# Gated differential attention on one core: two elementwise steps moved from VectorE to GpSimd

## The chip, the cores and the metric

The program runs on one core of a Trainium2 chip. A core has five engines that work side by side and wait for each other through semaphores: TensorE (PE, matmul; PEld is its weight load), VectorE (DVE), ScalarE (ACT), GpSimd (POOL) and SyncE (SP, which here only issues DMAs). Each engine works through its own instructions in one fixed order. The metric is device time in microseconds for one execution. Before the change it is 1170.07 us, the median of 3 runs (1167.32 to 1170.65).

## The reference

The layer is one pre-norm residual block over x (1024 tokens, width 1024). With 16 heads, each of two 64-wide query and key halves and 128-wide values:

```python
h = rms_norm(x, norm_g)
q, k, v, z = jnp.split(h @ w_in, 4, axis=-1)          # each 2048 wide
q = rms_norm(q.reshape(b, s, 16, 2, 64), q_norm_g) * 64 ** -0.5
k = rms_norm(k.reshape(b, s, 16, 2, 64), k_norm_g)
probs = softmax(q k^T - slope * distance, causal)      # two maps per head
o = (probs[:, :, 0] - lam * probs[:, :, 1]) @ v        # 128 wide per head
o = rms_norm(o, head_norm_g) * (1.0 - lam_0)
o = o.reshape(b, s, 2048) * jax.nn.silu(z)
return x + o @ w_out
```

The change touches two places: how w_in is prepared for TensorE, and the last product of a head, rms_norm(o, head_norm_g) * (1 - lam_0) * silu(z).

## The kernel before

**Numbers in two parts.** TensorE is fed 16-bit operands. Each fp32 matrix is split in a high part (the rounded value) and a low part (what the rounding left), and a product is three matmuls: high by high, high by low, low by high. So w_in has to be scaled and split before a head can be projected.

**Stages.** A prologue loads x, norms and transposes it, and prepares the first head's weights. Then the program goes through 16 heads (odd ones first). While head i is projected (`project`), head i-1 is attended (`attend`); `merge` interleaves the two generators by planned times, and a scheduler then orders each engine's instructions. At the end come the last gates and the output projection.

**`project`.** For each of 8 token blocks, 24 matmuls of 384 columns into `pg` (q, k and v together; lines 365 to 367). ACT copies `pg` to `rw` and `vh`, DVE makes `vl` (line 419). For each half of the tokens `norm` works on q and k: GpSimd multiplies q by a gain (line 380), DVE sums squares (L378), adds an eps (L95), scales (L383) and makes the low part (L387), and DMA transposes to `qk`. Then for each half of the tokens `gate` runs 24 matmuls of 512 columns into `pz` (lines 442 to 444), and a chain of ACT and DVE makes silu(z) in the tile `sz`: Exp L447, min L448, Ln L449, L450, Exp L451, and L452, which multiplies by `inv`, the factor that undoes the weights' scaling. `pg` and `pz` share three PSUM banks, so a new `pg` may have to wait until L452 has read an old `pz`.

**`split_w`.** The next head's w_in comes as `raww` (128 partitions, 8 pieces of the contraction, 4 blocks q, k, v, z of 128 columns). There is one buffer of it. ACT squares the blocks for their scale (L159), the scale is worked out in small steps, ACT writes the high parts (L197, one per block), and the low parts follow: for the blocks in `LO_POOL` (v and z) on GpSimd as a scaling in place (L200) and a subtraction (L201); for the others (q and k) on DVE in one instruction (L203). The next head's `raww` DMAs (L135, on SP's queue) can be issued when the last of these has read the buffer.

**`attend`.** 8 steps, one for each block of 128 queries. A step's scores go into `pss`, which has four PSUM banks: two maps, each in pieces of up to 512 keys (L564). DVE evacuates each piece with the bias added (L553), ACT takes Exp (L570), DVE combines the two maps (L576), ACT and DVE split the result (L66, L580), a DMA transposes it into `wt` (L582). After step 5 the first four blocks are multiplied by the values, the second four in the next head's stretch (L594 to L596). Each gives a tile of 512 tokens: `os`, its squares `sq`, and a split `sqh`, `sql` (GpSimd, L607) that TensorE sums over the partitions with two matmuls into `pmn` (L613, L614). ACT turns the sum into 1/rms (L616, L617), DVE multiplies `os` by the gain `gh` and by it (L624), and `finalize` multiplies by `sz` on GpSimd (L532) and stores to `g_dram`. Heads 10, 12 and 14 (`LATE`) get their gates at the very end; 10 and 12 use line 622 for their norm, and 14, the last, does its products on DVE.

Of the kernel before, what the change touches and what calls it, by code (L numbers as in the profile page):

```python
# [9 lines left out]
F32 = mybir.dt.float32  # L10
# [4 lines left out]
ALU = mybir.AluOpType  # L15
# [17 lines left out]
NORM_AT = 6  # L33
TAIL = (0, 1, 1, 0, 0, 0, 0, 0)
PSS, PSG = 4, 3
LO_POOL = (2, 3)


@with_exitstack
def diff_attention_kernel(  # L40
# [67 lines left out]
    with ExitStack() as main:  # L108
# [31 lines left out]
        def split_w(raw, blocks, wt, hd, first=False, pin=lambda ins: ins):  # L140


            if "both" not in wt:
                wt["both"] = wp.tile([P, 2, KT, 4, P], F16, name="wsp", tag="wsp")
                wt["hi"], wt["lo"] = wt["both"][:, 0], wt["both"][:, 1]
                wt["inv"] = wsm.tile([P, 2, 4], F32, name="inv", tag="inv", bufs=3)
            hi, lo, inv = wt["hi"], wt["lo"], wt["inv"]
            n, bs = len(blocks), slice(blocks[0], blocks[-1] + 1)
            bd = wsm.tile([P, 4], F32, name="bd", tag="bd")
            if first:  # L150
                b8 = wsm.tile([P, 3, KT], F32, name="b8", tag="b8", bufs=1)
                for k in range(KT):
                    pin(V.tensor_reduce(out=b8[:, :, k], in_=raw[:, k, bs], axis=AX.X, op=ALU.max,
                                        apply_absolute_value=True))
                    yield
                pin(V.tensor_reduce(out=bd[:, :n], in_=b8, axis=AX.X, op=ALU.max))
            else:
                for j, s_ in enumerate(blocks):
                    A.activation(hi[:, :, s_], raw[:, :, s_], AF.Square, accum_out=bd[:, j:j + 1])  # L159
                    yield  # L160
            br = wsm.tile([P, 4], F32R, name="br", tag="br")
            if n % 2:
                G.memset(br.bitcast(F32), 0.0)
            pin(V.tensor_scalar(br[:, :n], bd[:, :n], 1.0, None, ALU.mult))
            while wt["pb"] is None:
                yield
            pb = wt["pb"]()
            T.matmul(pb[:, :n + n % 2], ones, br[:, :n + n % 2], start=True, stop=True)
            top = wsm.tile([P, 4], F32, name="topw", tag="topw")
            top = top[:, :n]  # L170
            pin(V.tensor_scalar(top, pb[:, :n], float(P), 2.0 ** (-20 if first else -40), ALU.mult, ALU.max))
            if not first:
                A.activation(top, top, AF.Ln)
                A.activation(top, top, AF.Exp, scale=0.5)
            pin(V.tensor_scalar(top.bitcast(I32), top.bitcast(I32), 0x7F800000, None, ALU.bitwise_and))
            sc = wsm.tile([P, 4], F32, name="scw", tag="scw")
            sc = sc[:, :n]
            pin(V.reciprocal(sc, top))
            pin(V.tensor_scalar(sc, sc, 2.0 ** 14, None, ALU.mult))

            def rest():

                V.tensor_scalar(inv[:, 0, bs], top, sg[1], 2.0 ** -14, ALU.mult, ALU.mult)
                V.tensor_scalar(inv[:, 1, bs], inv[:, 0, bs], -1.0, None, ALU.mult)
                if blocks[0] == 0 and not isinstance(hd, slice):
                    ep = wsm.tile([P, 2], F32, name="ep", tag="ep")
                    V.tensor_tensor(ep, sc[:, :2], sc[:, :2], ALU.mult)
                    V.tensor_scalar(ep, ep, sg[2], unit_of(hd) ** 2, ALU.mult, ALU.mult)
                    wt["ep"] = ep

            if not first:
                rest()
            yield
            for ks in (slice(0, 4), slice(4, 8)) if first else (slice(0, 8),):
                for j, s_ in enumerate(blocks):
                    src, h_, l_, c_ = raw[:, ks, s_], hi[:, ks, s_], lo[:, ks, s_], sc[:, j:j + 1]
                    pin(A.activation(h_, src, AF.Copy, scale=c_))  # L197
                    yield
                    if s_ in LO_POOL:
                        pin(G.tensor_scalar(src, src, c_, 1.0, ALU.mult, ALU.mult))  # L200
                        pin(G.tensor_tensor(l_, src, h_, ALU.subtract))  # L201
                    else:
                        pin(V.scalar_tensor_tensor(out=l_, in0=src, scalar=c_, in1=h_,  # L203
                                                   op0=ALU.mult, op1=ALU.subtract))
                    yield
            if first:
                rest()

        def unit_of(hd):
            return 2.0 ** ((8 - (hd + 2) // 2) // 2 - 11)  # L210
# [3 lines left out]
        with ExitStack() as pro:  # L214
# [52 lines left out]
            for t in range(NB):  # L267
# [18 lines left out]
                if t == 4:  # L286
# [12 lines left out]
                    gh = cp.tile([P, 1], F32, name="gh")  # L299
                    Q.dma_start(gh, head_norm_g[:, None])  # L300
                    V.tensor_scalar(gh, gh, 1.0 - LAM0, None, ALU.mult)

                    V.tensor_tensor(gk, gain[:, 0], gk, ALU.mult)
                    ga = x1.tile([P, 64], F32, name="ga")
# [133 lines left out]
        def gate(st, wt, n, c):  # L438

            pz = ps_g.tile([P, 512], F32, name="pz", tag="pg")  # L440
            for k in range(KT):
                T.matmul(pz, wt["hi"][:, k, n], hh[c][:, k], start=k == 0, stop=False)  # L442
                T.matmul(pz, wt["hi"][:, k, n], hl[c][:, k], start=False, stop=False)  # L443
                T.matmul(pz, wt["lo"][:, k, n], hh[c][:, k], start=False, stop=k == KT - 1)  # L444
                yield k
            e = vp.tile([P, 512], F32, name="sz", tag="sz", bufs=3)
            A.activation(e, pz, AF.Exp, scale=wt["inv"][:, 1, n:n + 1])  # L447
            V.tensor_scalar(e, e, 1e18, None, ALU.min)  # L448
            A.activation(e, e, AF.Ln, bias=1.0)  # L449
            V.scalar_tensor_tensor(out=e, in0=pz, scalar=wt["inv"][:, 1, n:n + 1], in1=e, op0=ALU.mult, op1=ALU.max)  # L450
            A.activation(e, e, AF.Exp, scale=-1.0)  # L451
            V.scalar_tensor_tensor(out=e, in0=pz, scalar=wt["inv"][:, 0, n:n + 1], in1=e,  # L452
                                   op0=ALU.mult, op1=ALU.mult)
            st["z"].append(e)

# [79 lines left out]
        def attend(hd, st):  # L535
# [48 lines left out]
            def values(c, t):  # L584
# [20 lines left out]
                A.activation(sqh, os, AF.Square)  # L605
                sql = tmp.tile([P, 512], F32R, name="sql", tag="sql")
                e.tensor_tensor(sql, sq, sqh.bitcast(F32), ALU.subtract)  # L607
                pos["n"] = (os, sq, sqh, sql)

            def head_norm(c):  # L610
# [7 lines left out]
                if hd in LATE[:-1]:  # L618
                    nm = ("whz", "wlz")[c]
                    t1 = wzp.tile([P, 512], F32, name="t1", tag=nm)  # L620
                    st["t"].append(t1)
                    V.scalar_tensor_tensor(out=t1, in0=os, scalar=gh, in1=sq, op0=ALU.mult, op1=ALU.mult)
                else:
                    V.scalar_tensor_tensor(out=sq, in0=os, scalar=gh, in1=sq, op0=ALU.mult, op1=ALU.mult)  # L624
                    finalize(hd, c, sq, st["z"][c])

            ts = []
# [119 lines left out]
```

## Time and profile before

| | us |
|---|---|
| median of 3 runs | 1170.07 |
| the profiled execution's own time | 1169.15 |
| its span in the trace | 1167.4 |
| PE busy | 1109.9 (95%) |
| DVE busy | 906.5 (78%) |
| ACT busy | 751.7 (64%) |
| POOL busy | 269.7 (23%) |

The prediction is made against the profiled execution's own time, 1169.15 us. A matmul counts as busy until its last result is out, and the next one begins before that, so PE's busy share has no more to say than where PE stands still. What matters are the stretches where it does, and which instruction of another engine ended them. The trace's granted clock is 0.982 of full speed over the span.

### The profile page before, as it was taken

How to read it: one execution, taken by the hardware profiler on the slowest of the kernel's cores; microseconds unless marked ns; L12 is line 12 of the kernel's file. 1: busy time of each engine (PE TensorE's matmuls, PEld its weight loads, DVE VectorE, ACT ScalarE, POOL GpSimd, SP SyncE). 2: the span in 40 equal slices, each digit the busy share in tenths (PEclk: the TensorE clock that was granted, in tenths of full speed). 3: DMA queues.
4: the chain of work that ended last, by engine and by line, in shares of the span. 5: the costliest groups of instructions: out<-in, count | busy, mean ns of one | idle time of the engine just before them, and what ended most of it. 6: DMA issues, size and time to landing. Idle time of an engine off the chain costs nothing.

```text
span 1167.4 us, 18462 instructions
## 1 busy us (share of the span) xinstructions
PE 1109.9 (95%) x6154; PEld 670.2 (57%) x6154; DVE 906.5 (78%) x2336; ACT 751.7 (64%) x1585; POOL 269.7 (23%) x208
## 2 busy tenths in 40 slices
PE   4999999999899999999999999999999988999998
PEld 3655554555455555554545555555555535788887
DVE  6868968898879898989888989797898898554121
ACT  4757678686868686868686868686768766230000
POOL 2221313131413131314131313212120402022000
PEclk7999999999999999999999999999999988999999
DMA  6352636354636364635473635353664456766341
GB/s 222 109 118 57 147 82 143 81 125 96 142 84 141 86 144 83 150 77 145 82 150 77 147 80 136 79 142 70 138 136 91 116 112 160 193 235 227 113 131 70
DMA packets 327887, 143.50 MB, mean 123 GB/s; under 512 B 225136, under 2 KB 307312, under 8 KB 327792
## 3 DMA queue, kind: packets, MB, share of 16 engines
q1 hardware_dynamic: 323040, 133.93, 47.8%
q10 hardware_dynamic: 4752, 8.39, 2.6%
q8 instruction: 48, 0.79, 0.3%
q14 instruction: 47, 0.39, 0.1%
HBM read 63.11 MB, written 16.25 MB: 68 GB/s over the span
## 4 chain that ended last, share of the span: by engine, by line
PE 53%; DVE 15%; ACT 11%; DMA 7%; issue 6%; POOL 4%; SPq 4%; ACTq 0%; DVEq 0%; POOLq 0%
PE pg L365 8%; PE pg L366 8%; PE pg L367 8%; PE pf L493 5%; PE pf L494 5%; PE pf L495 5%; DMA raww<-in_l_w_in_dram 4%; DVE p L553 4%; SPq L135 3%; PE pss L564 3%; ACT wsp L197 3%; ACT wsp L159 3%; POOL wsp L201 2%; ACT p L570 2%; DVE p L576 2%
## 5 line engine op out<-in xcount | busy, mean ns | idle before, releaser
L365 PE MATMUL pg<-wsp,h 128*128 128x384 f16 x1024 | 336.1, 328 | 12.8 <-DVE sz L452 7.7
L366 PE MATMUL pg<-wsp,h 128*128 128x384 f16 x1024 | 336.1, 328 | 1.2 <-POOL wsp L201 1.2
L367 PE MATMUL pg<-wsp,h 128*128 128x384 f16 x1024 | 336.0, 328 | 0.9 <-DVE h L276 0.9
L570 ACT ACTIVATE p<-p,mn 128x128 f32<-128x128 f32 (+7 forms) x256 | 196.6, 769 | 36.1 <-DVE mn L553 36.0
L564 PE MATMUL pss<-qk 128*128 128x512 f16 (+3 forms) x768 | 165.9, 327 | 18.5 <-DVE mn L553 18.5
L553 DVE CUSTOM_DVE_ANT_0 p<-pss,toep,nsl 128x512 f32<-128x512 f32 (+3 forms) x256 | 161.3, 643 | 17.7 <-DMA wt<-p 8.2
L66 ACT ACTIVATE p<-p,rc 128x128 f16<-128x128 f32 (+7 forms) x128 | 98.8, 773 | 77.6 <-DVE p L576 71.7
L366 PEld LDWEIGHTS <-h 128*128 128x128 f16 x1024 | 100.8, 98 | 77.3 <-issue 17.2
L367 PEld LDWEIGHTS <-h 128*128 128x128 f16 x1024 | 100.8, 98 | 68.7 <-issue 4.0
L365 PEld LDWEIGHTS <-h 128*128 128x128 f16 x1024 | 100.7, 98 | 65.9 <-issue 3.7
L580 DVE SCALAR_TENSOR_TENSOR p<-p,rc,p 128x128 f16<-128x128 f32 (+7 forms) x128 | 109.1, 853 | 10.2 <-ACT p L66 9.4
L564 PEld LDWEIGHTS <-qk 128*128 128x128 f16 x768 | 70.8, 98 | 78.6 <-issue 26.6
L576 DVE SCALAR_TENSOR_TENSOR p<-p,rc,p 128x128 f32<-128x128 f32 (+7 forms) x128 | 108.7, 854 | 0.0
L607 POOL TENSOR_TENSOR sql<-sqo,sqh 128x512 fp32r<-128x512 f32 x30 | 41.0, 1366 | 263.2 <-ACT sqh L605 263.2
L442 PE MATMUL pz<-h,wsp 128*128 128x512 f16 x256 | 98.1, 383 | 1.8 <-DVE sz L452 1.8
L444 PE MATMUL pz<-h,wsp 128*128 128x512 f16 x256 | 98.1, 383 | 0.0
L443 PE MATMUL pz<-h,wsp 128*128 128x512 f16 x256 | 98.1, 383 | 0.0
L200 POOL TENSOR_SCALAR raww<-raww,scw 128x1024 f32<-128x1024 f32 (+1 forms) x31 | 43.5, 1410 | 178.4 <-ACT wsp L197 137.2
L532 POOL TENSOR_TENSOR sz<-sqo,sz 128x512 f32<-128x512 f32 x26 | 33.7, 1295 | 184.9 <-DVE sqo L624 165.4
L159 ACT ACTIVATE wsp<-raww 128x1024 f16<-128x1024 f32 x61 | 63.7, 1045 | 19.3 <-DMA raww<-in_l_w_in_dram 14.9
L553 DVE CUSTOM_DVE_ANT_0 p<-pss,toep,mn 128x128 f32<-128x128 f32 (+3 forms) x128 | 75.4, 603 | 0.3 <-PE pss L564 0.3
L201 POOL TENSOR_TENSOR wsp<-raww,wsp 128x1024 f16<-128x1024 f32 (+1 forms) x31 | 71.7, 2327 | 0.5
(159 smaller groups left out, 2048.7 us busy)
## 6 DMA issues: line engine op xcount, KB each, us to landing
raww<-in_l_w_in_dram SPq DMA_DIRECT2D x96, 256.0 KB, 4.3
rawo<-in_l_w_out_dram SPq DMA_DIRECT2D x32, 256.0 KB, 4.7
qk<-qk SPq DMA_DIRECT2D x64, 128.0 KB, 2.3
raww<-in_l_w_in_dram SPq DMA_DIRECT2D x40, 192.0 KB, 3.6
g_dram<-sz SPq DMA_DIRECT2D x30, 256.0 KB, 2.2
rawg<-g_dram ACTq DMA_DIRECT2D x24, 256.0 KB, 4.0
xt<-in_x_dram SPq DMA_DIRECT2D x8, 512.0 KB, 5.2
xr<-in_x_dram SPq DMA_DIRECT2D x16, 256.0 KB, 3.5
```

What stands on the lines that cost most here:

```text
L66: A.activation(out, in_, AF.Copy, scale=scale)
L159: A.activation(hi[:, :, s_], raw[:, :, s_], AF.Square, accum_out=bd[:, j:j + 1])
L365: T.matmul(pg, a_h, w_h, start=k == 0, stop=False)
L366: T.matmul(pg, a_h, w_l, start=False, stop=False)
L367: T.matmul(pg, a_l, w_h, start=False, stop=k == KT - 1)
L442: T.matmul(pz, wt["hi"][:, k, n], hh[c][:, k], start=k == 0, stop=False)
L443: T.matmul(pz, wt["hi"][:, k, n], hl[c][:, k], start=False, stop=False)
L553: V.tensor_tensor_reduce(out=pm[m][:, o:o + w], in0=pss[:, :w], in1=toep[:, u:u + w], scale=nslope, scalar=3e38 if prev[m] is None else pr ...
L564: T.matmul(pss[m][:, :w].rearrange("p (t q) -> p t q", q=P), qk[:, c, 0, i % 4, m], qk[:, b, v, :w // P, m], start=v == 1, stop=v == 2)
L570: A.activation(pm[m][:, :n], pm[m][:, :n], AF.Exp, scale=-1.0, bias=prev[m], accum_out=sx[:, m:m + 1])
L576: V.scalar_tensor_tensor(out=p0, in0=p1, scalar=rc[:, 1:2], in1=p0, op0=ALU.mult, op1=ALU.add)
L580: V.scalar_tensor_tensor(out=pl[:, n:], in0=p0, scalar=rc[:, 0:1], in1=pl[:, :n], op0=ALU.mult, op1=ALU.subtract)
```

## The change

The low part of the k block joins those of v and z on GpSimd, in all but the first head's first preparation. A new column `gi` holds `inv` of the z block times the head norm's gain, and L452 (now line 458) multiplies by it; so the gain is in `sz` already. In the 13 heads that are not in `LATE`, GpSimd multiplies `sz` by `os` (new line 615), and the product with 1/rms stays in `finalize` (old L532, now 538), directly on ACT's result. The DVE product of `os`, gain and 1/rms falls away there.

```diff
-LO_POOL = (2, 3)
+LO_POOL = (1, 2, 3)
...
                 V.tensor_scalar(inv[:, 1, bs], inv[:, 0, bs], -1.0, None, ALU.mult)
+                if blocks[-1] == 3:
+                    wt["gi"] = wsm.tile([P, 1], F32, name="gi", tag="gi", bufs=3)
+                    V.tensor_tensor(wt["gi"], inv[:, 0, 3:4], gain_h[0], ALU.mult)
...
-                    if s_ in LO_POOL:
+                    if s_ in LO_POOL and not (first and s_ < 2):
                         pin(G.tensor_scalar(src, src, c_, 1.0, ALU.mult, ALU.mult))
                         pin(G.tensor_tensor(l_, src, h_, ALU.subtract))
...
+        gain_h = []
...
                     V.tensor_scalar(gh, gh, 1.0 - LAM0, None, ALU.mult)
+                    gain_h.append(gh)
...
-            V.scalar_tensor_tensor(out=e, in0=pz, scalar=wt["inv"][:, 0, n:n + 1], in1=e,
+            V.scalar_tensor_tensor(out=e, in0=pz, scalar=wt.get("gi", wt["inv"][:, 0, n:n + 1]), in1=e,
                                    op0=ALU.mult, op1=ALU.mult)
...
                 e.tensor_tensor(sql, sq, sqh.bitcast(F32), ALU.subtract)
+                if hd not in LATE:
+                    G.tensor_tensor(st["z"][c], os, st["z"][c], ALU.mult)
                 pos["n"] = (os, sq, sqh, sql)
...
+                elif hd == heads[-1]:
+                    V.scalar_tensor_tensor(out=sq, in0=os, scalar=gh, in1=sq, op0=ALU.mult, op1=ALU.mult)
+                    finalize(hd, c, sq, st["z"][c])
                 else:
-                    V.scalar_tensor_tensor(out=sq, in0=os, scalar=gh, in1=sq, op0=ALU.mult, op1=ALU.mult)
                     finalize(hd, c, sq, st["z"][c])
```

The scheduler orders every engine's instructions anew. Lines behind the new ones have other numbers: L451, L452, L553, L576, L580, L582 are now 457, 458, 559, 582, 586, 588; L200 and L201 are 203 and 204; L380, L387 and L607 are 386, 393 and 613.

**VectorE, from one head into the next.** Before, between q and k's low part (`sqk`) and the evacuation of step 1's scores (256 keys):

```order
L387 TENSOR_TENSOR sqk<-rw,sqk 128x16x64
L576 SCALAR_TENSOR_TENSOR p_4870<-p_4871,rc,p_4870 128x1024
L624 SCALAR_TENSOR_TENSOR sqo<-os,gh,sqo 128x512
L553 ISA p_5000,mn<-pss,toep,nsl 128x256
L553 ISA mn 128x1
L553 ISA p_5001,mn<-pss,toep,nsl 128x256
L553 ISA mn 128x1
L452 SCALAR_TENSOR_TENSOR sz<-pz,inv,sz 128x512
```

Now, at the same place of a later head:

```order
L458 SCALAR_TENSOR_TENSOR sz<-pz,gi,sz 128x512
L579 RECIPROCAL rc<-sx 128x2
L559 ISA p_5649,mn<-pss,toep,nsl 128x128
L559 ISA mn 128x1
L559 ISA p_5650,mn<-pss,toep,nsl 128x128
L559 ISA mn 128x1
L580 TENSOR_SCALAR rc<-rc,sx,nlam 128x1
L583 TENSOR_SCALAR rc<-rc,wsc 128x1
L393 TENSOR_TENSOR sqk<-rw,sqk 128x16x64
L582 SCALAR_TENSOR_TENSOR p_5571<-p_5572,rc,p_5571 128x1024
L559 ISA p_5701,mn<-pss,toep,nsl 128x256
```

The head norm's product is gone from in front of the evacuations, and the gate's last product (`sz` from `pz`) stands ahead of them and not behind.

**ScalarE, the same place.** Before, the gate's last Exp (L451) stands behind three of the four squares of the next weights:

```order
L616 ACTIVATE sqo<-pmn,eps_t 128x512
L386 ACTIVATE sqk<-rw 128x16x64
L617 ACTIVATE sqo<-sqo 128x512
L159 ACTIVATE wsp,bd<-raww 128x8x128 x3
L451 ACTIVATE sz<-sz 128x512
L159 ACTIVATE wsp,bd<-raww 128x8x128
```

Now:

```order
L457 ACTIVATE sz<-sz 128x512
L624 ACTIVATE sqo<-pmn,eps_t 128x512
L576 ACTIVATE p_6328,sx<-p_6328,mn 128x128
L625 ACTIVATE sqo<-sqo 128x512
L392 ACTIVATE sqk<-rw 128x16x64
L576 ACTIVATE p_6329,sx<-p_6329,mn 128x128
L66 ACTIVATE p_6250<-p_6249,rc 128x1024
L576 ACTIVATE p_6380,sx<-p_6380,mn 128x256
L159 ACTIVATE wsp,bd<-raww 128x8x128 x2
```

That Exp is now ahead of the squares, with seven other instructions between.

**GpSimd, one head's weights and what follows.** Before:

```order
L200 TENSOR_SCALAR raww<-raww,scw 128x8x128 x2
L201 TENSOR_TENSOR wsp<-raww,wsp 128x8x128 x2
L380 TENSOR_TENSOR rw<-rw,gain 128x512
L607 TENSOR_TENSOR sql<-sqo,sqh 128x512
L532 TENSOR_TENSOR sz<-sqo,sz 128x512
```

Now, in every second head (in the others the product of `os` and `sz` stands behind the third subtraction and the gain):

```order
L204 TENSOR_TENSOR wsp<-raww,wsp 128x8x128
L203 TENSOR_SCALAR raww<-raww,scw 128x8x128
L204 TENSOR_TENSOR wsp<-raww,wsp 128x8x128
L615 TENSOR_TENSOR sz<-os,sz 128x512
L204 TENSOR_TENSOR wsp<-raww,wsp 128x8x128
L386 TENSOR_TENSOR rw<-rw,gain 128x512
L613 TENSOR_TENSOR sql<-sqo,sqh 128x512
L538 TENSOR_TENSOR sz<-sqo,sz 128x512
```

In front of these rows stand two scalings (L203). So the last reader of `raww` has one scaling, one subtraction and, in these heads, one product more ahead of it, and `sql` too.

**SyncE's queue at the same time.** Before:

```order
L582 DMA_TRANSPOSE wt_5297<-p_5296 128x10x128
L582 DMA_TRANSPOSE wt_5297<-p_5346 128x12x128
L135 DMA raww<-in_l_w_in_dram 128x4x128 x8
L582 DMA_TRANSPOSE wt_5297<-p_5458 128x14x128
L388 DMA_TRANSPOSE qk<-sqk 128x16x128
```

Now, in every second head:

```order
L588 DMA_TRANSPOSE wt_5322<-p_5321 128x10x128
L135 DMA raww<-in_l_w_in_dram 128x4x128
L588 DMA_TRANSPOSE wt_5322<-p_5371 128x12x128
L135 DMA raww<-in_l_w_in_dram 128x4x128 x7
L588 DMA_TRANSPOSE wt_5322<-p_5484 128x14x128
```

Step 5's transpose (12x128) has a load of the next weights in front of it, which waits for GpSimd's last subtraction.

## Rows read from the trace of the kernel before

**Rows 1.** Busy time by stretch: us, PE, PEld, DVE, ACT, POOL, clock, DMA, GB/s.
```profile
198.00:742.00 544.00, 525.86 (x3057) 293.85 (x3056) 467.37 (x1233) 416.38 (x883) 140.84 (x94) 1.00 0.51 113
...
842.00:990.00 148.00, 134.77 (x705) 72.20 (x704) 132.89 (x343) 105.21 (x220) 32.56 (x24) 0.95 0.55 124
```

**Rows 2.** PE's waits, 198 to 742: us in total, times, longest.
```profile
PE pss L564 <- DVE mn L553: 9.1, 9, 1.6
PE pg L365 <- DVE sz L452: 7.3, 8, 1.9
```

**Rows 3.** Timeline of PE around 492: start, us, instruction [idle before, releaser].
```profile
492.17 1.02 PE L564 MATMUL pss<-qk 128*128 128x512 f16 x4 [0.76 <-DVE mn L553]
494.02 0.32 PE L365 MATMUL pg<-wsp,h 128*128 128x384 f16 x1 [0.83 <-DVE sz L452]
```

**Rows 4.** Timeline of DVE ahead of these waits.
```profile
488.65 1.21 DVE L387 TENSOR_TENSOR sqk<-rw,sqk 128x1024 f16<-128x1024 f32 x1
489.78 1.27 DVE L576 SCALAR_TENSOR_TENSOR p<-p,rc,p 128x1024 f32<-128x1024 f32 x1
490.97 0.74 DVE L624 SCALAR_TENSOR_TENSOR sqo<-os,gh,sqo 128x512 f32<-128x512 f32 x1
491.63 0.47 DVE L553 CUSTOM_DVE_ANT_0 p<-pss,toep,nsl 128x256 f32<-128x256 f32 x1
...
493.22 0.75 DVE L452 SCALAR_TENSOR_TENSOR sz<-pz,inv,sz 128x512 f32<-128x512 f32 x1 [0.70 <-ACT sz L451]
```

**Rows 5.** The chain that ended last, 470 to 496: start, us, what.
```profile
476.63 2.14 POOL wsp L201
...
478.78 0.61 SPq L135
...
483.56 5.34 DMA raww<-in_l_w_in_dram
...
489.43 3.23 ACT wsp L159 x6
492.66 0.53 ACT sz L451
```

**Rows 6.** DVE's groups by line and shape: count, busy us, mean ns, idle before.
```profile
L624 DVE SCALAR_TENSOR_TENSOR sqo<-os,gh,sqo 128x512 f32<-128x512 f32 x28 | 20.9, 748 | 4.9 <-ACT sqo L617 4.7
L203 DVE SCALAR_TENSOR_TENSOR wsp<-raww,scw,wsp 128x1024 f16<-128x1024 f32 x32 | 40.2, 1296 | 1.4 <-ACT wsp L197 1.4
L187 DVE TENSOR_TENSOR ep<-scw 128x2 f32<-128x2 f32 x16 | 2.5, 154 | 0.0
```

**Rows 7.** POOL's groups by line and shape.
```profile
L201 POOL TENSOR_TENSOR wsp<-raww,wsp 128x1024 f16<-128x1024 f32 x29 | 69.0, 2398 | 0.3
...
L200 POOL TENSOR_SCALAR raww<-raww,scw 128x1024 f32<-128x1024 f32 x29 | 40.6, 1408 | 157.5 <-ACT wsp L197 137.2 <-DMA wt<-p 20.3
L532 POOL TENSOR_TENSOR sz<-sqo,sz 128x512 f32<-128x512 f32 x26 | 33.7, 1295 | 184.9 <-DVE sqo L624 165.4 <-DVE rc L573 14.2 <-DVE scw L178 5.3
```

**Rows 8.** Timeline of DVE, 460 to 520: three instructions that meet POOL or don't.
```profile
460.43 1.85 DVE L387 TENSOR_TENSOR sqk<-rw,sqk 128x1024 f16<-128x1024 f32 x1
...
477.78 2.23 DVE L95 TENSOR_SCALAR v_k<-ssk,ep 128x8 f32<-128x8 f32 x2
...
513.78 0.36 DVE L95 TENSOR_SCALAR v_k<-ssk,ep 128x8 f32<-128x8 f32 x2
```

**Rows 9.** Timeline of POOL, the same stretch.
```profile
459.93 1.27 POOL L532 TENSOR_TENSOR sz<-sqo,sz 128x512 f32<-128x512 f32 x1 [4.24 <-DVE sqo L624]
...
473.83 4.93 POOL L201 TENSOR_TENSOR wsp<-raww,wsp 128x1024 f16<-128x1024 f32 x2
478.72 1.26 POOL L380 TENSOR_TENSOR rw<-rw,gain 128x512 f32<-128x512 f32 x1
```

**Rows 10.** SP's timeline, the same stretch.
```profile
486.05 1.89 SPq L582 DMA_TRANSPOSE wt<-p  x1
```

**Rows 11.** A wait of DVE, the whole run: us in total, times, longest.
```profile
DVE p L553 <- DMA wt<-p: 8.2, 8, 2.5
```

## Prediction

> **What bounds the kernel now.** The busy time by stretch comes first. From 198 to 742 us nine heads run in the same pattern; PE is busy 525.86 of 544 us there, DVE 467.37 (86%), ACT 416.38, POOL 140.84 [rows 1]. So TensorE is the bound, and a change on other engines is worth at most the 18.1 us in which PE stands still there, and its like in the neighbouring stretches. PE's waits say what ended that idle time: the reader is to see two lines that make 16.4 of it, 9.1 us for DVE's evacuation of scores (9 times) and 7.3 us for the end of the gate (8 times) [rows 2]. The timeline shows the two side by side in one head: 0.76 us before step 3's scores, then 0.83 us before the next projection [rows 3]. DVE's timeline shows what stands ahead of them: q and k's low part, the combination of step 7, the head norm's product, and only then the evacuation of step 1 [rows 4]. The chain of waits tells where the second comes from: GpSimd's last subtraction ends at 478.77, the next weights' loads are issued from 478.78 on, the last lands near 488.9, ACT squares them until 492.66, and only then takes the Exp that the gate's last product, and so PE, waits for [rows 5].
>
> **What goes from VectorE.** In 13 heads the product L624 goes, twice a head: 26 x 0.748 = 19.4 us [rows 6]. The k block's low part L203 goes for 16 of 32 instructions: 16 x 1.296 = 20.7 us [rows 6]. 13 one-column products for `gi` come; their nearest row is the two-column L187 at 0.154: 2.0 us [rows 6]. DVE is relieved by 38.1 us, 2.64 us in a full head (2 x 0.748 + 1.296 - 0.154).
>
> **What comes to GpSimd.** 26 products like L532 at 1.295 us make 33.7 us; 16 scalings at 1.408 and 16 subtractions at 2.398 make 60.9 us [rows 7]. That is 94.6 us more, 6.4 us in a full head. GpSimd was busy 140.84 of 544 us [rows 1], so it has the room; what counts is where the new work lies and whom it holds up.
>
> **What the two do to each other.** Beside GpSimd, some DVE instructions last longer. L387 takes 1.85 us where it starts inside an L532 of GpSimd, and 1.21 us alone [rows 4, 8, 9]: 0.64 more. The two L95 take 2.23 us where GpSimd's L201 and L380 run, and 0.36 us without [rows 8, 9]: 1.87 more. L532 ended 0.77 us after L387 had begun (459.93 + 1.27 against 460.43), about the time lost, and the L95 pair ends at 480.01, when L380 does (479.98). So a DVE instruction of these kinds stands still until the running GpSimd instruction is over. Per head that is 2.5 us for about 15.6 us of GpSimd (140.84 over nine heads [rows 1]), or 0.16 us per us. The price of the added 94.6 us lies between nothing (no such DVE instruction falls into it) and 58 added instructions x 0.94 us (1.87 over two) = 54.5 us. I take the ratio, since it holds both hits and misses of the same mix: 15.1 us. DVE's net relief is then 38.1 - 15.1 = 23.0 us, about 1.6 us a head (2.64 - 6.4 x 0.16), out of the range from +16 to -38.
>
> The Trainium skill (SBUF — State Buffer, section "Who interferes with whom") has the rule behind this: VectorE with two SBUF inputs and GpSimd reading SBUF share a port that is held for a whole instruction, and the second to start fully blocks. The 0.64 and 1.87 us agree with it; by the rule alone the change would be paid at the upper end, which is the third case below.
>
> **The wait on the evacuation.** L624 holds the evacuation back by 0.66 us (490.97 to 491.63) out of a wait of 0.76 [rows 3, 4]. In the new order it is gone from there. PE's order changes too: between the scores of 256 and of 512 keys in steps 1 to 3 stood 12 projection matmuls; now there are 36, all ahead of the 384-key step or 24 of them behind it. Four of 512 columns take 1.02 us [rows 3], so 24 of 384 give DVE about 4.6 us more (24 x 1.02 / 4 x 384 / 512). So I expect these 9.1 us to go.
>
> **The wait on the gate.** The Exp now stands ahead of the squares, so it no longer waits for the next weights to land, and the last product stands ahead of step 7's combination. The 7.3 us should go as well, though another `pg` or `pz` may then come late: the row that waits already is L451 with 0.70 of DVE idle [rows 4].
>
> **The later release of the weights.** The last subtraction comes later by one scaling and one subtraction, 3.8 us, and in every second head by a product of 1.3 us; the first scaling can start one block of ACT earlier (about 1.1 us), so 2.7 to 4.0 us. The squares have moved back behind seven instructions, which covers that on ACT. On SP the loads are ahead of transposes: the last load was issued by about 484.2 and the next transpose at 486.05 [rows 5, 10], a cover of 1.9 us. What is left, 0.8 to 2.1 us, makes a transpose late; its price is in the case on the weights below, and I take nothing for it here. The sum over the partitions in `pmn` gets its low part later by the same queue; the new order puts that matmul near the end of the gate, so I take nothing for it either.
>
> **The sum.** Between 198 and 742 us the removed waits are worth 16.4 us at most. How much of it comes back as waits elsewhere no row can show: the bounds are none and all. I take half, because DVE stays over 80% busy (467 less 9 x 1.6 of 544) and PE still has only four banks of scores. Elsewhere PE's idle time is mostly 842 to 990 us (148 - 134.77 = 13.2 us [rows 1]), where only two or three heads lose one L203 each; I take nothing. So 1169.15 - 8.2 = 1161 us. The profiled execution's time is 0.9 us under the median of the runs shown, which I neglect.
>
> **The other cases.**
>
> No change: DVE's relief is used up by the blocking, and the two waits move elsewhere in full. For it: the relief is no larger than 1.6 us a head, and the pattern of PE's waits comes from in-order queues, which are all new. Against it: both named waits lose their named cause. Time: 1169 us, within 0.3% (about 3.5 us, what a measurement of this kernel can tell from no change).
>
> Slower by blocking: the weights' burst on GpSimd, 7.6 us before (two blocks of 1.408 + 2.398 [rows 7]), is 11.4 us now and lies in steps 5 to 7, where DVE combines and splits the longest rows with two inputs from SBUF and runs L95. If nearly every added instruction stops one of these for 0.94 us, DVE gets 54.5 - 38.1 = 16.4 us longer. It decides from 2.8 of the 4 added instructions in a head on (2.64 / 0.94). With half of that on PE's path, 1169 + 8 = 1177 us. Against it: one head's 15.6 us of GpSimd cost only 2.5 us before.
>
> Slower by the late weights: a load that waits for GpSimd holds SP's queue, step 5's and step 6's transposes start late, and the buffers of `p` come free late for the next head's steps. Such a wait stands in the trace with 8.2 us in 8 times, 1.0 us each [rows 11]. It decides where the last subtraction ends after the split of step 5 (768 keys). At one such wait more in each of 15 heads and no gain kept, 1169 + 15 = 1184 us; with half the gain kept, 1176 us. Against it: the split of step 5 itself stands later in the new order.
>
> **Chances.** Faster, as forecast, 0.62; the case's own range is 1150 (all 16.4 us and a few from the neighbouring stretches) to 1166. No change 0.14. Slower by blocking 0.13, by the late weights 0.11. So faster 0.62, same 0.14, slower 0.24. The range that leaves 2 in 10 out goes from 1150, all waits gone, to 1177, into the two slower cases.
>
> **What would show it.** Right: PE's waits between 198 and 742 us fall from 16.4 to about 8 us, with the evacuation's nearly gone; DVE's busy time falls by about 23 us and POOL's grows by about 95 us; L624's successor has a count of 2. Wrong: DVE's busy time falls by under 10 us with longer L95, L582 or L586 (blocking), or DVE's evacuation waits for `wt<-p` far over 8.2 us, or ACT's squares for the weights (late weights), or PE waits for `sql`. If PE's idle time in the nine heads falls by half and the time doesn't, the step that sums it up is wrong.

## The result, and the profile after

The changed kernel takes 1211.98 us (median of 4 runs, 1211.49 to 1215.22); the kernel before takes 1168.69 (1167.24 to 1170.65). The ratio is 1.0368 with a 95% interval of 1.0343 to 1.0394, so the change makes the kernel 3.7% slower. The forecast was 1161 us, faster, with a range of 1150 to 1177: the time moved the other way and past that range. Of all executions behind this document two lie apart from the others of their kernel, one of 2971.61 us with the k block in the old order and one of 1191.42 with the products in it, and no trace of these two is read.

The busy times of the profile after say first what kind of loss it is:

```profile
PE 1119.8 (93%) x6154; PEld 671.3 (55%) x6154; DVE 898.7 (74%) x2307; ACT 751.7 (62%) x1585; POOL 358.8 (30%) x266
```

The span grew from 1167.4 to 1209.7, by 42.3 us. PE's busy time grew by 9.9 us (from 1109.9) with the same 6154 matmuls; the other 32.4 us is PE standing still. DVE's busy time, which was to lose about 23 us, lost 7.8 (from 906.5), while POOL grew by 89.1.

PE's four longest waits between 198 and 742 us of the profile after (us in total, times, longest):

```profile
PE pg L371 <- DVE vl L425: 21.4, 8, 4.7
PE pss L570 <- DVE mn L559: 5.5, 8, 1.2
PE po L600 <- issue: 3.7, 1, 3.7
PE pg L371 <- DVE sz L458: 2.5, 8, 0.5
```

The two waits that the change was to remove did shrink, from 9.1 to 5.5 and from 7.3 to 2.5 us [rows 2]. A new one of 21.4 us took their place: the projection waits for a `pg` bank, which DVE frees when it has made `vl`. ACT's timeline in one such head (start, us, instruction, idle before it) shows why `vl` is late:

```profile
506.41 1.04 ACT L392 ACTIVATE sqk<-rw 128x1024 f16<-128x1024 f32 x1
509.31 1.06 ACT L159 ACTIVATE wsp<-raww 128x1024 f16<-128x1024 f32 x1 [1.86 <-DMA raww<-in_l_w_in_dram]
...
512.45 1.04 ACT L159 ACTIVATE wsp<-raww 128x1024 f16<-128x1024 f32 x1
...
513.48 0.61 ACT L625 ACTIVATE sqo<-sqo 128x512 f32<-128x512 f32 x1
...
514.77 1.13 ACT L66 ACTIVATE p<-p,rc 128x1024 f16<-128x1024 f32 x1
515.81 0.36 ACT L423 ACTIVATE rw<-pg 128x256 f32<-128x256 f32 x1
516.08 0.26 ACT L424 ACTIVATE vh<-pg 128x128 f16<-128x128 f32 x1
```

The four squares of the next weights (L159) stand in one piece ahead of the copies L423 and L424 that empty `pg`. ACT first waits 1.86 us for the weights to land, then squares for 4.2 us; behind the squares stand the head norm, two short Exps and a split (L66), and the copies come at 515.81. DVE makes `vl` behind them, and PE, which could have gone on at 512.8, goes on at 517.48. PE's timeline and two windows from there on (window, length, busy times and counts of PE, PEld, DVE, ACT, POOL, granted clock, DMA share, GB/s):

```profile
517.48 0.48 PE L371 MATMUL pg<-wsp,h 128*128 128x384 f16 x1 [4.71 <-DVE vl L425]
```
```profile
517.40:521.00 3.60, 3.52 (x12) 1.67 (x12) 3.26 (x13) 3.29 (x10) 0.00 (x0) 0.53 0.78 150
521.00:524.60 3.60, 3.60 (x24) 2.14 (x22) 2.91 (x10) 2.47 (x8) 0.00 (x0) 1.00 0.26 53
```

After PE stood still for 4.71 us the granted clock is 0.53, close to its lower level (1.2 of 2.4 GHz), and in 3.6 us 12 matmuls pass instead of the 24 that pass in the next 3.6. So behind this wait the matmuls themselves are slower, which counts as PE's busy time and not as waiting.

Why the weights land late is seen on POOL and SP of the same head, here one after the other:

```profile
484.43 3.06 POOL L203 TENSOR_SCALAR raww<-raww,scw 128x1024 f32<-128x1024 f32 x2 [7.25 <-ACT wsp L200]
...
491.38 4.22 POOL L204 TENSOR_TENSOR wsp<-raww,wsp 128x1024 f16<-128x1024 f32 x2
```
```profile
495.63 0.61 SPq L135 DMA_DIRECT2D raww<-in_l_w_in_dram  x1
496.45 1.45 SPq L588 DMA_TRANSPOSE wt<-p  x1
497.95 4.85 SPq L135 DMA_DIRECT2D raww<-in_l_w_in_dram  x7
```

The burst takes 11.2 us (484.43 to 495.60; before 7.7, 471.04 to 478.77). The first load goes out right behind it, but the other seven stand behind a transpose on SP's queue, so the last is issued by 502.80, 7.2 us behind the burst (5.4 before, 478.78 to 484.18). And DVE has an instruction beside the burst:

```profile
493.41 3.01 DVE L586 SCALAR_TENSOR_TENSOR p<-p,rc,p 128x768 f16<-128x768 f32 x1
```

This instruction, the low part of a step's result, takes 3.0 us in five heads, and 1.01 us at 441.20, in the head before this one. Two more waits grew over the whole program: DVE's evacuation for `wt<-p` (23.7 us in 19 times, where 8.2 stood [rows 11]) and ACT's squares for the weights (25.1 us, where 14.9 stood). So three suspects stand in the trace: the new order of ACT's queue, DVE held back by GpSimd, and weights that land late. The experiments take them apart.

### The profile page after: what moved, and what is told of

The parts are those of the page before. It is cut to its first block, busy times and chain, and to the rows that moved or that the text cites. A ratio compares the mean times of both kernels' runs of the same rounds, so it can differ in the third digit from the quotient of the medians.

```text
span 1209.7 us, 18483 instructions
## 1 busy us (share of the span) xinstructions
PE 1119.8 (93%) x6154; PEld 671.3 (55%) x6154; DVE 898.7 (74%) x2307; ACT 751.7 (62%) x1585; POOL 358.8 (30%) x266
## 4 chain that ended last, share of the span: by engine, by line
PE 43%; DVE 24%; DMA 11%; ACT 10%; issue 9%; SPq 3%; POOL 1%; DVEq 0%; ACTq 0%; POOLq 0%
PE pg L371 7%; PE pg L372 7%; PE pg L373 7%; DVE p L559 6%; PE pf L499 5%; PE pf L500 5%; PE pf L501 5%; DMA wt<-p 4%; DMA raww<-in_l_w_in_dram 4%; DVE p L586 3%; ACT wsp L159 3%; DVE p L582 2%; PE pss L570 2%; SPq L135 2%; ACT p L576 2%
## 5 line engine op out<-in xcount | busy, mean ns | idle before, releaser
L576 ACT ACTIVATE p<-p,mn 128x128 f32<-128x128 f32 (+7 forms) x256 | 196.4, 769 | 68.7 <-DVE mn L559 67.7
L559 DVE CUSTOM_DVE_ANT_0 p<-pss,toep,nsl 128x512 f32<-128x512 f32 (+3 forms) x256 | 160.8, 642 | 40.3 <-DMA wt<-p 23.7
L66 ACT ACTIVATE p<-p,rc 128x128 f16<-128x128 f32 (+7 forms) x128 | 98.7, 772 | 73.8 <-DVE p L582 71.5
L586 DVE SCALAR_TENSOR_TENSOR p<-p,rc,p 128x128 f16<-128x128 f32 (+7 forms) x128 | 117.5, 918 | 13.9 <-ACT p L66 13.7
L582 DVE SCALAR_TENSOR_TENSOR p<-p,rc,p 128x128 f32<-128x128 f32 (+7 forms) x128 | 117.3, 917 | 0.0
L570 PEld LDWEIGHTS <-qk 128*128 128x128 f16 x768 | 71.4, 98 | 75.3 <-issue 20.9
L203 POOL TENSOR_SCALAR raww<-raww,scw 128x1024 f32<-128x1024 f32 (+1 forms) x47 | 66.5, 1422 | 140.3 <-ACT wsp L200 120.0
L615 POOL TENSOR_TENSOR sz<-os,sz 128x512 f32<-128x512 f32 x26 | 36.5, 1403 | 227.0 <-ACT os L606 227.0
L204 POOL TENSOR_TENSOR wsp<-raww,wsp 128x1024 f16<-128x1024 f32 (+1 forms) x47 | 100.9, 2153 | 0.2
L159 ACT ACTIVATE wsp<-raww 128x1024 f16<-128x1024 f32 x61 | 63.6, 1045 | 25.1 <-DMA raww<-in_l_w_in_dram 25.1
L600 PE MATMUL po<-wt,vh 128*128 128x512 f16 x192 | 64.0, 333 | 14.7 <-DMA wt<-p 6.0
```

The lines of the kernel that those rows point to most:

```text
L66: A.activation(out, in_, AF.Copy, scale=scale)
L559: V.tensor_tensor_reduce(out=pm[m][:, o:o + w], in0=pss[:, :w], in1=toep[:, u:u + w], scale=nslope, scalar=3e38 if prev[m] is None else pr ...
L570: T.matmul(pss[m][:, :w].rearrange("p (t q) -> p t q", q=P), qk[:, c, 0, i % 4, m], qk[:, b, v, :w // P, m], start=v == 1, stop=v == 2)
L576: A.activation(pm[m][:, :n], pm[m][:, :n], AF.Exp, scale=-1.0, bias=prev[m], accum_out=sx[:, m:m + 1])
L582: V.scalar_tensor_tensor(out=p0, in0=p1, scalar=rc[:, 1:2], in1=p0, op0=ALU.mult, op1=ALU.add)
L586: V.scalar_tensor_tensor(out=pl[:, n:], in0=p0, scalar=rc[:, 0:1], in1=pl[:, :n], op0=ALU.mult, op1=ALU.subtract)
```

## Halves of the change, and the squares put later

The first two runs do one half each. In the first, only the line `LO_POOL` is put back; in the second, only the k block goes to GpSimd (in the kernel before).

```diff
-LO_POOL = (1, 2, 3)
+LO_POOL = (2, 3)
```

> The changed kernel with the k block's low part back on VectorE; the folded gain and both products on GpSimd stay. Late weights (three blocks on GpSimd release the single buffer of raw weights late, and the squares that wait for the reload stand on ScalarE in front of the projection's copies): PE's wait on vl goes, time 1160 to 1175 us. Blocking (GpSimd's instructions stop VectorE's, whichever they are): the products are 33.7 of 94.6 us of the added GpSimd work, so about a third of the 43 us stays, 1180 to 1188 us. Products at fault (the product of os and sz in front of sql): over 1200 us.

Measured: 1195.16 (1191.26 to 1198.79), ratio 1.0225 [1.0184, 1.0266]. That lies between two of the expectations (up to 1188, and over 1200). The products alone lose 25 us, and PE waits for `vl` again (22.6 us over the whole run). The burst is back to two blocks, and in this head ACT's squares run without a wait (ACT's timeline):

```profile
442.80 1.04 ACT L159 ACTIVATE wsp<-raww 128x1024 f16<-128x1024 f32 x1
...
445.91 1.04 ACT L159 ACTIVATE wsp<-raww 128x1024 f16<-128x1024 f32 x1
...
448.29 0.37 ACT L423 ACTIVATE rw<-pg 128x256 f32<-128x256 f32 x1
449.59 0.27 ACT L424 ACTIVATE vh<-pg 128x128 f16<-128x128 f32 x1
```

They stand ahead of the copies all the same, so the squares come to this place in the queue without late weights.

```diff
-LO_POOL = (2, 3)
+LO_POOL = (1, 2, 3)
...
-                    if s_ in LO_POOL:
+                    if s_ in LO_POOL and not (first and s_ < 2):
```

> The kernel before with the k block's low part on GpSimd (not in the first head's preparation) and nothing else. Late weights: the slow part is here, 1200 to 1215 us, with PE waiting on vl by 15 us or more. Blocking: two thirds of the 43 us, 1192 to 1200 us. Products at fault: 1165 to 1175 us.

Measured: 1199.41 (1194.55 to 1201.38), ratio 1.0259 [1.0225, 1.0292]. The other half alone loses 30 us, as the expectation by blocking has it. 25 and 30 are more than 43: the two losses are not independent.

Next the squares are taken off their place: each is queued behind one more copy to `vh`, in the changed kernel and in the kernel before.

```diff
-                            A.activation(vh[:, c * 4 + t], pg[:, 256:], AF.Copy, scale=vsc)
+                            copied.append(A.activation(vh[:, c * 4 + t], pg[:, 256:], AF.Copy, scale=vsc).ins)
...
-                    A.activation(hi[:, :, s_], raw[:, :, s_], AF.Square, accum_out=bd[:, j:j + 1])
+                    with (tc.issue_after(copied[-1]) if copied else ExitStack()):
+                        A.activation(hi[:, :, s_], raw[:, :, s_], AF.Square, accum_out=bd[:, j:j + 1])
```

> The changed kernel, with each of the four squares of the next weights queued on ScalarE behind one more copy of the projection (vh of blocks 0 to 3), so that no square can stand in front of the copy that frees the first PSUM bank. GpSimd's work is untouched. Late weights: PE's wait on vl falls under 6 us and the time to 1170 to 1188 us. Blocking or products at fault: 1200 us or more, since GpSimd and VectorE do what they did.

> The same queueing of the squares in the kernel before. Late weights: the squares also delay the gate's last Exp there, so its 7.3 us of PE's waits between 198 and 742 us go, time 1158 to 1166 us. Blocking or products at fault says nothing of it: 1166 to 1172 us.

Measured: the changed kernel 1185.77 (1183.6 to 1187.85), ratio 1.0148 [1.012, 1.0176]; the kernel before 1151.69 (1147.09 to 1153.51), ratio 0.985 [0.9818, 0.9883]. The wait for `vl` is gone and 26 us come back, though PE now waits 21.8 us over the run for the gate's last product (11 times). But the same step also helps the kernel before, by 18 us, and the gap between the two is still 34 us. The kernel before with late squares is the fastest version of this study, and it has nothing of the change in it.

With late squares the halves were run again, then the fold with its products on VectorE (the same place in the program, no new work on GpSimd), and the opposite of the change, one block less on GpSimd:

```diff
-                    G.tensor_tensor(st["z"][c], os, st["z"][c], ALU.mult)
+                    V.tensor_tensor(st["z"][c], os, st["z"][c], ALU.mult)
```

> The changed kernel with the late squares, but the k block's low part on VectorE as before: only the fold and the 26 products on GpSimd are left of the change. To be set against the kernel before with late squares (1151.7) and the whole change with late squares (1185.8), 34 us apart. Theory 1 (GpSimd's instructions hold DVE back, in proportion to their time): the products are 33.7 of the 94.6 us added, so 36% of the 34: about 1164. Theory 2 (the weights released later): the products add little to the burst, so about 1152 to 1156, and ACT's squares wait for raww no more than the 14 to 15 us of the kernel before. Theory 3 (the place of the products in the program, ahead of the norm, whatever engine does them): most of the 34 us stay, 1175 or more.

> The kernel before with late squares and with the k block's low part on GpSimd, without fold and products: the other half. Theory 1 (held back in proportion to GpSimd's time): 60.9 of 94.6 us, so 64% of the 34 us: about 1173. Theory 2 (the weights released later): nearly all of the 34 us, 1180 to 1186, with ACT's squares waiting for raww by 20 us or more. Theory 3 (the products' place): none of it, 1150 to 1155.

> As the run with late squares and products only, but the 26 products are done by VectorE at the same place of the program: the gain is folded, GpSimd does what it does in the kernel before, and VectorE has as many two-input instructions as before. Theory 1 (what GpSimd does beside VectorE is the cost): 1152 within 5, and DVE's time beyond the unhindered as in the kernel before with late squares. Theory 3 (the place of the products ahead of the norm): as slow as the run with the products on GpSimd, 1164 or more.

> The kernel before with late squares and with only one block's low part (instead of two) on GpSimd, the other on VectorE: the opposite step of the change's, 61 us less on GpSimd, 21 to 25 us more on DVE. Theory 1: if GpSimd's time costs DVE more than it relieves it of, this is as fast as or faster than 1151.7, down to 1140. Where 0.16 us per us held, as in the prediction, DVE would have 10 to 15 us more to do net, and the time would be 1152 to 1165.

Measured: products 1199.05 (ratio 1.0242 [1.0208, 1.0275]), k block 1169.64 (0.9986 [0.9966, 1.0005]), fold on VectorE 1212.47 (1.0358 [1.0324, 1.0391]), one block less 1158.26 (0.9892 [0.9852, 0.9931]). The k block comes near the proportional split (1173), but the products miss it (1164) by 35 us and alone are slower than both halves together (1186). And the fold on VectorE is as slow as the whole change with nothing new on GpSimd. One block less on GpSimd cannot be told from the kernel before with late squares (the intervals of the two ratios overlap), so it decides nothing. Two readings are left: the products cost by their place in the program, whatever engine does them (theory 3), or with each edit the scheduler deals new queues whose quality swings by tens of us. PE of the run with the products, at the end of a head, and DVE beside it:

```profile
502.25 0.48 PE L573 MATMUL pss<-qk 128*128 128x384 f16 x2 [0.70 <-DVE mn L562]
504.86 0.49 PE L573 MATMUL pss<-qk 128*128 128x384 f16 x2 [2.12 <-DVE mn L562]
```
```profile
502.12 1.28 DVE L585 SCALAR_TENSOR_TENSOR p<-p,rc,p 128x1024 f32<-128x1024 f32 x1
503.32 1.22 DVE L396 TENSOR_TENSOR sqk<-rw,sqk 128x1024 f16<-128x1024 f32 x1
504.45 0.34 DVE L562 CUSTOM_DVE_ANT_0 p<-pss,toep,nsl 128x128 f32<-128x128 f32 x1
```

No instruction here is stretched. DVE has the combination of step 7 and q and k's low part queued ahead of an evacuation of 0.34 us that PE stands still for.

## The work and the order apart

From here on the order is held. The rows of PE, ACT, DVE and SP of one kernel were put into another as a table (`ORDER`), and edges that set the order of issue alone chain the instructions; what DVE loses is left out of its row, what it gains stands behind the neighbour that it has in its own kernel. GpSimd's row is left free, so whatever its own order costs counts as work here.

```diff
...
         diff_attention_kernel(tc, *args)
+        at = {i.name: i for i in nc.cur_bb.bb.instructions}
+        for row in zlib.decompress(base64.b85decode(ORDER)).decode().split(";"):
+            names = [f"I-{n}" for n in accumulate(map(int, row.split(",")))]
+            for a, b in zip(names, names[1:]):
+                tc.add_manual_dep(at[b], a, mybir.DependencyInfo(mybir.DependencyClass.NoSync,
+                                                                    mybir.DependencyReason.DATA), reason="order")
```

> The changed kernel, all of its work, but the instructions of PE, ACT, DVE and SP are held in the order that they have in the kernel before (edges that set the order of issue alone); what the change takes from DVE is left out of its row, the 13 products for gi are put in, and GpSimd gets its new instructions. Theory 1 (the re-ordering of the queues is the loss): no slower than before, 1150 to 1169, about the predicted 1161. Theory 2 (GpSimd's work holds DVE back, or lets the next weights go too late): the work is all there, so 1195 to 1212. If only the squares' place on ACT counts, about 1186.

> The reverse: the kernel before, all of its work on the engines where it was, but PE, ACT, DVE and SP in the order of the changed kernel (the products and low parts that DVE keeps stand in their old neighbourhood). Theory 1: the loss comes without the change, 1195 or more, with PE waiting for vl behind the squares. Theory 2: 1165 to 1175.

> All of the change's work in the order of the kernel before with late squares (1151.7). Theory 1: DVE's relief may help a little more, 1140 to 1153. Theory 2: as the changed kernel with late squares, 1180 to 1190.

> Only the fold and the products on GpSimd (the k block's low part on DVE), in the order of the kernel before with late squares. The same work in its own order took 1199. Theory 1: 1143 to 1153, and the difference to the run before this one is what the k block's low part is worth in a fixed order. Theory 2: 1164 to 1199.

With what the halves gave (below), the times are:

| work | its own order | old order | changed kernel's order | order with late squares |
|---|---|---|---|---|
| as before | 1168.69 to 1171.32 | same | 1197.40 | 1151.69 |
| whole change | 1211.98 | 1232.90 | same | 1192.91 |
| products | 1195.16 | 1175.60 | not run | 1174.31 |
| k block | 1199.41 | 1225.85 | not run | not run |

The ratios to the kernel before are 1.0522 [1.0487, 1.0557] for the change in the old order, 1.0221 [1.0189, 1.0253] for the old work in the new order, 1.0177 [1.0146, 1.0208] for the change in the order with late squares, and 1.0027 [1.0009, 1.0045] for the products in it. Here theory 1 is the order of the queues, theory 2 the work itself. Neither survives alone. The new order costs 26 us with none of the new work, and PE's waits (198 to 742 us of that run) show the same new wait:

```profile
PE pg L420 <- DVE vl L474: 13.6, 9, 2.1
PE pss L619 <- DVE mn L608: 9.4, 5, 2.9
```

(Line numbers in these runs are 53 to 66 higher, because the table stands ahead of the code.) But the work costs more still, 62 us, where the order stays as it was, and 41 us in the order with late squares. In the old order PE waits for DVE's evacuation, over the whole run 40.0 us in 25 times against 18.5 in 17 before (here this run, then the kernel before):

```profile
PE pss L626 <- DVE mn L615: 40.0, 25, 3.5
```
```profile
PE pss L564 <- DVE mn L553: 18.5, 17, 2.3
```

PE's busy time is also 28.0 us longer with the same matmuls (1137.9), at a granted clock of 0.958 over the span (0.982 before). And DVE is seen beside POOL:

```profile
459.93 2.28 DVE L638 SCALAR_TENSOR_TENSOR p<-p,rc,p 128x1024 f32<-128x1024 f32 x1
```
```profile
459.18 1.95 POOL L594 TENSOR_TENSOR sz<-sqo,sz 128x512 f32<-128x512 f32 x1 [6.99 <-ACT sqo L681]
```

The combination took 1.27 us in the kernel before [rows 4]. In the order with late squares it is GpSimd's own queue that is late: `sql` stands behind the longer burst and the new product of `os` and `sz`, and PE waits for it, 20.9 us in 11 times:

```profile
PE pmn L675 <- POOL sql L666: 20.9, 11, 5.1
```

So the scheduler's new order was even an improvement for the new work (1233 to 1212). And the same products cost 6 us in the old order and 23 in the one with late squares (over 1151.69), against 47 where the scheduler was free: their place in the program alone does not make the loss. What is left to explain is the price of the work itself.

## Holding back and late weights, each alone

Two runs add one suspect each to the kernel before, in its own order. The first gives GpSimd an idle pair of the k block's size, on a scratch tile, once `raww` is free. In the second ACT reads one column of `raww` ahead of the gate's Exp in ten heads, which lets the loads start at 438.92 instead of 437.01, the end of GpSimd's burst.

```diff
...
+            if not first and blocks[0] == 0:
+                with tc.issue_after(last.ins):
+                    G.tensor_scalar(d32, d32, one, 1.0, ALU.mult, ALU.mult)
+                    G.tensor_tensor(d16, d32, d16, ALU.subtract)
```
```diff
...
+            if hd in heads[3:13]:
+                rd = wsm.tile([P, 1], F32, name="rd", tag="rd")
+                A.activation(rd, raw[:, 0, 0, :1], AF.Copy)
```

> The kernel before, in its own order on PE, ACT, DVE and SP, with one more scaling and one more subtraction on GpSimd a head, of the size of the k block's, on a scratch tile, behind the last instruction that reads raww. They hold back nothing by data: what they cost is DVE held back beside them and GpSimd's own next instructions later by up to 3.8 us. Theory A (holding back is the price, with the change's work in the old order 62 us over before): 1185 to 1205. Theory B (the price is the later release of raww): 1168 to 1176.

> The kernel before, in its own order, with one column of raww read by ACT ahead of the gate's first Exp in ten heads, so that the next weights' loads can start at about 480.8 instead of 478.8 us of the trace, 2 us later, as they do in the change in the old order; nothing is added on GpSimd. Theory A: 1170 to 1175. Theory B: up to the whole 2 us in each of ten heads, 1185 to 1192.

Measured: idle pair 1201.83 (1201.49 to 1203.81), ratio 1.0268 [1.0243, 1.0293]; late read 1199.90 (1196.31 to 1201.47), ratio 1.0244 [1.0214, 1.0273]. Each alone costs the kernel before about the same, 32 and 30 us. The busy times of the run with the idle pair:

```profile
PE 1122.5 (94%) x6154; PEld 672.1 (56%) x6154; DVE 938.2 (78%) x2336; ACT 753.5 (63%) x1585; POOL 333.2 (28%) x243
```

DVE has the same 2336 instructions as before and is busy 31.7 us longer, beside 63.5 us more of POOL: half a us per us. (PE's busy time is 12.6 us longer too, with the same matmuls.) Part of DVE's loss falls on the smallest instructions. DVE and POOL in that run, then the whole group:

```profile
438.00 2.10 DVE L157 SCALAR_TENSOR_TENSOR v_k<-v_k,y_k 128x16 f32<-128x16 f32 x1
```
```profile
437.08 2.99 POOL L271 TENSOR_TENSOR d<-d,d 128x1024 f16<-128x1024 f32 x1
```
```profile
L157 DVE SCALAR_TENSOR_TENSOR v_k<-v_k,y_k 128x16 f32<-128x16 f32 x32 | 20.0, 626 | 0.5
```

A product of 16 columns ends at 440.10, with the subtraction beside it (440.07). In the kernel before the mean of this group was 170 ns. The Trainium skill (SBUF — State Buffer, section "Who interferes with whom") says that a DVE instruction with two SBUF inputs and a GpSimd instruction that reads SBUF share a port, and that one of them waits for the whole of the other. These rows agree. (GpSimd's `sql` also comes 1.1 us later in this run, behind the scaling of the pair, so it isn't holding back alone.)

In the run with the late read DVE is as busy as before (908.4), and ACT waits for the weights 29.9 us instead of 14.9. SP, ACT and PE of one head:

```profile
438.92 5.44 SPq L192 DMA_DIRECT2D raww<-in_l_w_in_dram  x8
444.46 3.73 SPq L642 DMA_TRANSPOSE wt<-p  x1
```
```profile
448.85 1.06 ACT L216 ACTIVATE wsp<-raww 128x1024 f16<-128x1024 f32 x1 [1.70 <-DMA raww<-in_l_w_in_dram]
...
451.98 0.61 ACT L511 ACTIVATE sz<-sz 128x512 f32<-128x512 f32 x1
```
```profile
450.43 1.11 PE L624 MATMUL pss<-qk 128*128 128x512 f16 x4 [0.76 <-DVE mn L613]
453.44 0.32 PE L425 MATMUL pg<-wsp,h 128*128 128x384 f16 x1 [1.89 <-DVE sz L512]
```

The chain is that of [rows 5], 1.9 us later: loads, squares, the gate's Exp, its product, the next `pg`. PE's wait is 1.89 us, where it was 0.83 in the head of [rows 3]. That is 1.1 us, yet each of the ten heads pays 3.0 on average (30 us in all). More than half of it is the clock (window, length, busy times, clock):

```profile
453.50:456.00 2.50, 2.50 (x11) 1.28 (x11) 1.52 (x6) 2.50 (x10) 0.00 (x0) 0.66 0.80 206
456.00:458.50 2.50, 2.50 (x11) 1.27 (x10) 2.50 (x10) 1.72 (x6) 0.00 (x0) 0.66 0.24 50
458.50:461.00 2.50, 2.50 (x18) 1.50 (x16) 1.48 (x6) 1.79 (x6) 0.00 (x0) 1.00 1.01 193
```

11 matmuls instead of 18 in each of two windows. Over the run PE's busy time is 1126.1 us, 16.2 more than before with the same matmuls, out of 29.8 us that the span grew. The two waits make the rest, 13.7 us more than in the kernel before: 15.4 us for the gate's product (7.7 there) and 24.5 for the evacuation (18.5 there), here of this run:

```profile
PE pss L624 <- DVE mn L613: 24.5, 22, 2.2
PE pg L425 <- DVE sz L512: 15.4, 10, 2.5
```

The two halves in the old order follow:

> The k block's low part on GpSimd, without fold and products, in the order of the kernel before. Both causes are in it and DVE has 20.7 us less to do. If A and B add, its time is 1171 and the excess of the run with the idle pair and half as much again as that of the late read (15 heads instead of ten), less up to 21. In its own order this work took 1199.

> Fold and products on GpSimd, the k block's low part on DVE, in the order of the kernel before. With the run before this one it splits the 62 us of the whole change in the old order. In its own order this work took 1195; in the order with late squares it was 22 us over its base, so about 1190 to 1195 if products cost about the same in any order, and 1171 or less if they cost something only together with the k block.

Measured: k block 1225.85 (1223.74 to 1225.90 in four executions), ratio 1.0463 [1.0433, 1.0493]; products 1175.60 (1171.01 to 1191.42), ratio 1.0044 [1.0022, 1.0067]. The k block pays 56 us. By the rule set down beforehand it should pay 32 for holding back, one and a half times 30 for the weights, less up to 21 for DVE's relief: 56 to 77. The measured 56 is its lower end. How late the weights are in this run is not seen, so the split of the 56 between the two causes is argued and not shown. The products pay 6, and together that is the 62 us of the whole change.

## Why the prediction was wrong, point by point

**PE as the bound, and the two waits.** Right. PE stayed the bound, and both waits shrank as their causes went (16.4 to 8.0 us, the 8 that the forecast gave).

**The step that failed: "The squares have moved back behind seven instructions, which covers that on ACT", with the release of the weights taken at nothing.** The text looked at the seven instructions ahead of the squares and not at those behind them. Behind them stand the copies that free `pg`: the squares had been waited for by an Exp, and now they were waited for by PE's projection. That is 21.4 us in eight waits. That the order alone brings this wait is shown (13.6 us in nine waits, and 1197 us, with all work where it was); that a later release costs PE more than its own length is shown too (2 us later, 3.0 us paid). The rival on the late weights named the place, raww's release, but priced it along SP's transposes at 1.0 us a head, not along ACT. Its sign there did come: DVE's evacuation waits 23.7 us for `wt<-p` where 8.2 stood. That the loads themselves would stand behind a transpose was not in it.

**Holding back, 15.1 us at 0.16 us per us.** Mis-sized. In the changed kernel DVE's busy time fell by 7.8 us where 38.1 were taken off it, so 30.3 us came back on 89.1 us of POOL: 0.34. With the order held it is 0.50. The ratio was taken from two places of one head over all of GpSimd's work, much of which lies where DVE is not disturbed; the added work lies in the burst, where the low part above takes 3.0 us in five heads. Of the two hits that the prediction sets beside the rule on two inputs, the 0.64 us is of that kind; the L95 pair (1.87) reads one tensor each, so it is a hit by the rows alone. The rival priced this well for the k block (0.94 us an instruction; the idle pair gave 31.7 over 32 instructions, 0.99), but counted on half of it reaching PE. In the old order the time grew by as much, 32.1 us; that sum also holds the later `sql` and PE's longer busy time, so how much of it is DVE's is not shown.

**Half of the gain comes back.** More came than went, since the new order brought a wait of its own.

**Which share is whose.** The new order costs 26 us with the old work and saves 21 with the new, so the 43 us have no single split. What is shown is each price where the order of the other four engines is held; GpSimd's own order was not. That the products are dear with late squares in the scheduler's own order (1199) and half as dear in the order held (1174, over 1152) is shown; by which rule the scheduler comes to its queues was not tried.

## What to carry to other kernels

Where a scheduler deals the queues, an edit is two changes, and the second can be the larger: hold the order, run the new work in it, and run the old work in the new order, before a gain or a loss is put down to the work. In a moved instruction's queue, look at who stands behind it and who waits for that. And work handed to an idle engine is free only if it neither lengthens a chain that frees a buffer nor stands beside instructions that it holds up.

## What was not expected of the hardware

The granted clock made up over half of the late read's price: after waits of 0.76 and 1.89 us it was 0.66 over 5 us (matmuls of 384 columns 0.32 us apart from 454.50 to 457.38, 0.16 ahead of that and behind), while after 0.76 and 0.83 us in the kernel before the same matmuls (L365 to L367, from 494.02) stay 0.16 us apart. It is not the length of one wait alone: in the run with the idle pair PE stood still for 2.98 us at 446.22, and the clock is 1.00 in the 7.5 us behind it. What decides it is open. And a DVE instruction on 16 columns took 2.10 us beside GpSimd, over ten times its mean in the kernel before.
